# Queries, keys and values by 512 columns, one gate unit in each iteration of a recurrent mixer, and later sums of weights

## The chip, the cores and the metric

The kernel runs on one core of a Trainium2 chip. A core has five engines that work side by side: TensorE (PE) multiplies matrices, VectorE (DVE) and ScalarE (ACT) work elementwise, GpSimd (POOL) does some elementwise work and issues copies, SyncE (SP) issues most transfers. TensorE's weight loads (PEld) are recorded apart from its matmuls (PE). The metric is the device time of one execution in microseconds (us), lower is better.

## The reference, cut to what matters

One sequence of 1024 tokens of width 1024 goes through two layers in float32.

```python
def recurrent_mixer(hn, w_in, conv_w, conv_b, ..., w_out):
    z = hn @ w_in                                   # 1024 -> 2 * 1408
    gate, xr = jnp.split(z, 2, axis=-1)
    xr = causal_depthwise_conv(xr, conv_w, conv_b)
    y = rg_lru(xr, gate_a_w, ..., lam)              # 16 blocks of 88 channels
    return (y * jax.nn.gelu(gate)) @ w_out

def rg_lru(x, w_a, b_a, w_x, b_x, lam):
    r = jax.nn.sigmoid(einsum("bsnd,nde->bsne", xb, w_a) + b_a)
    i = jax.nn.sigmoid(einsum("bsnd,nde->bsne", xb, w_x) + b_x)
    a = jnp.exp((-LRU_C * r) * jax.nn.softplus(-lam))
    u = sqrt(-expm1(2 * log_a)) * (i * x)           # then h[t] = a[t] h[t-1] + u[t]

def shared_kv(h, c_act, ...):
    hn = modulate(rms_norm(h, kv_norm_g), shift, scale)
    k, v = jnp.split(hn @ kv_w, 2, axis=-1)         # 1024 -> 2 * 1024, k normalised per head

def chunk_attention(hn, w_q, ...):
    q = rms_norm((hn @ w_q).reshape(...), q_norm_g) # 1024 -> 1024
    ...                                             # 16 chunks of 64 against 9 chunks of keys
    return out @ w_o

def sqrelu_mlp(hn, w1, w2):
    return jnp.square(jax.nn.relu(hn @ w1)) @ w2    # 1024 -> 4096 -> 1024
```

Layer 0 is the recurrent mixer and an MLP; then keys and values are formed from the residual stream; layer 1 is attention and an MLP. Shifts, scales and gates of both layers ("modulation") come from a product of one vector with large weights (`ada_w`, `kv_ada_w`).

## The kernel before, in words

**Precision.** Every large product is three matmuls, recorded at lines L329 to L331 in `mm3`: high times high, high times low, low times high. Each float32 operand is split into a high half by a copy on ScalarE (L196 for weights and reloaded activations) and the rest by a subtraction on VectorE (L200).

**The stream of weights.** A class `Stream` (`ws`) keeps one list of items in the order in which they are wanted. Loads are issued on SyncE's queue in that order, into a ring of seven raw buffers of 128x1024 (`ws.ns`). Items for TensorE (`to="w"`) are split into tiles `wh` and `wl`; there are eight such tiles, so four items can be split at a time (`cap["w"] = 8`). `ws.next()` gives the next split item, `ws.done()` frees its tiles and lets the next be split. Items of kind "a" are reloaded activations whose halves are tiles of 128x512; `cap["a"]` bounds how many of these may be held. Items of kind "u" are the modulation weights: each 128x1024 tile is multiplied with the vector and summed by one VectorE instruction (L362); `some(n)` puts n of them into the list. Items of kind "p" form sums of four quarter weights for the MLP (L126), some on VectorE, some on GpSimd.

**Two ways of order.** Queries, keys and values, and attention, are ordered by an automatic scheduler from the program's order and its dependencies. The mixer and both MLPs are ordered by hand: `tick()` counts steps of TensorE (12 matmuls of 512 columns in the mixer), `at(d, f)` puts work d ticks later, and `ws.lag[kind]` is how many ticks after a load was issued its first use is put into the program.

**The mixer.** The width of 1408 is 11 tiles (`NT`) of 128 channels. `xr(t)` projects tile t of the recurrent half (two halves of 512 tokens, 8 k-steps, 3 matmuls each: 48 matmuls), then the convolution (L924), copies of channel blocks on GpSimd (L932), and splits on ScalarE (L938) and VectorE (L945) follow some ticks later. `gate(t)` projects tile t of the gate half, also 48 matmuls. `recur(_done(t))` does the blocks of 88 channels that end in tile t: block products (12 matmuls of 88x512 for each block), sigmoids (L971), tanh, roots and exponentials on ScalarE, and multiplies and the scan on VectorE (L976, L995 to L1002). The scanned block goes to a tile of 128 channels by a transfer, is multiplied with its gate (L1015, `gated`), stored to DRAM (`ygd`) and loaded back as a split item.

The main loop over t = 4 to 10 runs `xr(t)`, `recur(_done(t - 1))` and a gate unit, except at t = 8, where no gate unit runs; gate units 8 and 9 come at t = 9 and 10, gate unit 10 and the last blocks' `recur` after the loop. The splits of a tile come a tick later where `late` holds (tiles 3 to 9 except 8).

**Output projection.** For each j of 4 output pairs, `part_of` multiplies the weights `w_out(0, j)` with three gated tiles and `w_out(1, j)` with four, for two halves of tokens and two output tiles: four banks, 36 and then 48 matmuls. Then `chunk` adds the last four gated tiles for all outputs. `cap["a"]` is 14 from the last gate unit on.

**MLP.** The first product is 16 steps p of seven products of quarter matrices; partial results are added on VectorE (L1263) in the first and L1285 in the second product. At step (13, 0) `ws.lag["p"]` goes from 4 to 2 ticks.

**Queries, keys and values.** Tokens are stationary (128 tokens by 128 k) and weights stream by 256 columns. One item holds four k-steps of 256 columns; a group is 256 output columns, two items. A bank of 128x512 holds two token tiles of one group. For queries' first two groups the two first token halves run k by k in four banks while the normalisation of the rest (`head`, L556 to L585) goes on; all else runs bank by bank. `tokens_out` copies a bank in two pieces of 128x256 (L1392), and for queries and keys squares it (L1395) and reduces it per head (L1396). `kvmodulate` forms the keys' and values' operand from the residual stream in three parts between query groups.

Of the kernel before, what the change touches and what calls it, by code (L numbers as in the profile page):

```python
# [10 lines left out]
AF = mybir.ActivationFunctionType  # L11
ALU = mybir.AluOpType
# [4 lines left out]
KD = 8  # L17
W = 1408
NT = 11
# [284 lines left out]
def trunk(ctx: ExitStack, tc: tile.TileContext, I, out, dbg=None, stop=None):  # L304
# [107 lines left out]
    for t in range(4, NT):  # L412
        w_in(NT + t)
        some({8: 3, 9: 2, 10: 3}.get(t, 0))
        gate_item(_done(t - 1))
        if t != 8:
            w_in(t if t < 8 else t - 1)
    w_in(NT - 1)
    gate_item(_done(NT - 1))
# [89 lines left out]

    mlp_units(0)  # L510
    for g in range(4):
        for kk in range(2):
            ws.add(I["wq"][g * 2 + kk], 1024)
    for g in range(8):
        for kk in range(2):
            ws.add(I["wkv"][g * 2 + kk], 1024)
        some(4)
    some(99)
# [430 lines left out]
    def conved(t):  # L949

        conv(t)
        at(1, copies, t)
        late = 2 < t < NT - 1 and t != 8
        at(4 if late else 3, split_hi, t)
        at(5 if late else 4, split_lo, t)
# [112 lines left out]
    gate(3)  # L1068
    for t in range(4, NT):
        xr(t)  # L1070
        recur(_done(t - 1))
        if t != 8:
            gate(t if t < 8 else t - 1)
    ws.cap["a"] = 14
    gate(NT - 1)
    recur(_done(NT - 1))
    h = []
# [25 lines left out]
    for j in range(4):  # L1103
# [4 lines left out]
        for c, ys in enumerate((ygits[:3], ygits[3:7])):  # L1108
            for ps, (half, e) in zip(pss, chunks):
                part_of(ps, its[c], e, half, ys, c == 0, c == 1)  # L1110
                if c:
                    into_h(2 * j + e, half, ps)
                elif j == 0 and half == 0:
                    load_h(2)
                tick()
            at(1, ws.done, its[c])
    ws.live["a"] -= 14
    ws.cap["a"] = 8
# [45 lines left out]
    def mlp_body(l, h, nrm, nxt, last):  # L1164
# [88 lines left out]
        for p in range(2, 16):  # L1253
# [14 lines left out]
            def after(x, p=p, ca=ca, cb_=cb_):  # L1268
                ws.run()
                if x == 6:  # L1270
                    store(p, ca, cb_)
                if (p, x) == (13, 0):
                    ws.lag["p"] = 2
# [113 lines left out]

    def tokens_out(dst, sq, g, t2, ps):
        tt = slice(2 * t2, 2 * t2 + 2)
        for e in range(2):  # L1390
            d = dst[2 * g + e].rearrange("p (t c) -> p t c", t=8)[:, tt, :]
            A_.activation(out=d, in_=ps[:, :, e * 128 : (e + 1) * 128], func=AF.Copy)  # L1392
        if sq is not None:
            t = slot()
            A_.activation(out=t[:, :HALF], in_=ps.rearrange("p a b -> p (a b)"), func=AF.Square)  # L1395
            V.tensor_reduce(  # L1396
                out=ssq[:, sq, tt, 4 * g : 4 * g + 4],
                in_=t[:, :HALF].rearrange("p (t n d) -> p t n d", t=2, n=4),
                axis=AX, op=ALU.add)

    def token_mm(ps, N, its, t2, e, k, start, stop):
        q = slice((2 * t2 + e) * 128, (2 * t2 + e + 1) * 128)
        it = its[k // 4]
        c = slice((k % 4) * 256, (k % 4) * 256 + 256)
        mm3(ps[:, e, :], N.hh[k][:, q], N.hl[k][:, q], it["hi"][:, c], it["lo"][:, c], start, stop)

    def tokens(dst, N, sq, g, its, half):

        for t2 in range(2 * half, 2 * half + 2):
            ps = bank((128, 2, 256))  # L1410
            for e in range(2):
                for k in range(KD):
                    token_mm(ps, N, its, t2, e, k, k == 0, k == KD - 1)
            tokens_out(dst, sq, g, t2, ps)

    def tokens2(dst, N, sq, g):
        its = [ws.next() for _ in range(2)]
        for half in range(2):
            tokens(dst, N, sq, g, its, half)
        for it in its:  # L1420
            ws.done(it)

# [3 lines left out]

    its = [[ws.next() for _ in range(2)] for _ in range(2)]
    todo = [(g, t2, bank((128, 2, 256))) for g in range(2) for t2 in range(2)]
    for k in range(KD):
        for g, t2, ps in todo:  # L1430
            for e in range(2):
                token_mm(ps, n3, its[g], t2, e, k, k == 0 and e == 0, k == KD - 1 and e == 1)
        head(k, n3)
    for g, t2, ps in todo:
        tokens_out(qt, 0, g, t2, ps)
    for g in range(2):
        tokens(qt, n3, 0, g, its[g], 1)
        for it in its[g]:
            ws.done(it)
    kvmodulate((0, 1, 2))  # L1440
    tokens2(qt, n3, 0, 2)
    kvmodulate((3, 4, 5))
    tokens2(qt, n3, 0, 3)
    kvmodulate((6, 7))
    kt_ = [slot() for _ in range(8)]
    for g in range(4):
        tokens2(kt_, KV, 1, g)
    rqk = cp.tile([128, 2, 8, 16], F32, name="rqk")
# [23 lines left out]
    vt = [slot() for _ in range(8)]  # L1472
    for g in range(4):
        tokens2(vt, KV, None, g)
        if g < 2:
            head_norms(g, (qt, kt_)[g])
    dump("q", qt)
# [239 lines left out]
def layouts(inputs):  # L1717
# [61 lines left out]
    def grouped(w):  # L1779
        u = units(w, 4, 256)  # L1780
        n = u.shape[0] // 2
        return np.stack([u[:n], u[n:]], 1).reshape(2 * n, 128, 1024)

# [32 lines left out]
```

## Time and profile before

| | |
|---|---|
| median of 3 executions | 2364.78 us (2363.08 to 2367.6) |
| the profiled execution's own time | 2363.05 us |
| its span in the profile | 2361.2 us |
| mean granted TensorE clock | 0.991 |
| PE / PEld / DVE / ACT / POOL busy, of the span | 96 / 82 / 74 / 53 / 17% |
| mixer with its output projection | 0 to about 484 us |
| first MLP | to 1119.6 us |
| queries, keys, values | 1119.6 to 1399.6 us |
| attention and its output projection | to about 1730 us |
| second MLP | to the end |

A group in the profile reads: line, engine, operation, what is written from what is read, shape, count, then total busy time and the mean in ns of one, then the idle time of that engine just before such instructions and what ended it. In a timeline, each row has its start, its length and, in brackets, idle time before it with the instruction that ended the wait. A matmul's recorded length contains its way through the array; what counts for throughput is the distance between starts.

### The profile page before, as it was taken

To read this page: it belongs to the slowest core of one execution; us is meant where nothing else is said; L and a number is where in the kernel's file an instruction comes from. 1 tells how busy PE (TensorE), PEld (TensorE's weight loads), DVE (VectorE), ACT (ScalarE), POOL (GpSimd) and SP (SyncE) were. 2 spreads that over 40 slices of the span, in tenths; PEclk is the share of its full clock that TensorE was granted. 3 is DMA by queue.
4 is the path that set the end of the run, shared out by engine and by line. 5 is a ranking of instruction groups with operands and counts; after the bars stand their busy time and mean duration, and the time that the engine had idled before them with its cause. 6 is when DMAs were issued, how large, how long until landed. Compare 5 with 4: busy or idle time off the path is not lost.

```text
span 2361.2 us, 31725 instructions
## 1 busy us (share of the span) xinstructions
PE 2272.8 (96%) x11740; PEld 1929.1 (82%) x11740; DVE 1749.7 (74%) x2580; ACT 1240.2 (53%) x2051; POOL 399.2 (17%) x419
## 2 busy tenths in 40 slices
PE   3999999999999899999999999999999999999999
PEld 2878787878887678888999999998888888778887
DVE  8688889588777877777764739996386565877775
ACT  5587883375555633344433239996275555634332
POOL 0000100000000033331000148874000000033332
PEclk9999899999999999999999999999999999999999
DMA  8225349226676865545444100014114445865543
GB/s 314 72 83 155 116 158 340 99 85 231 245 257 225 306 224 155 159 159 185 124 134 143 55 12 11 10 53 143 67 54 160 162 170 172 288 237 160 153 150 130
DMA packets 141639, 363.46 MB, mean 154 GB/s; under 512 B 14924, under 2 KB 17100, under 8 KB 141484
## 3 DMA queue, kind: packets, MB, share of 16 engines
q1 hardware_dynamic: 113756, 278.45, 35.5%
q10 hardware_dynamic: 23824, 71.44, 8.1%
q0 software_dynamic: 3904, 11.54, 1.9%
q8 instruction: 92, 1.51, 0.3%
q14 instruction: 63, 0.52, 0.1%
HBM read 260.19 MB, written 89.65 MB: 148 GB/s over the span
## 4 chain that ended last, share of the span: by engine, by line
PE 63%; DVE 9%; DMA 8%; ACT 7%; issue 3%; POOL 1%; ACTq 0%; SPq 0%; DVEq 0%; POOLq 0%
PE b L329 20%; PE b L331 20%; PE b L330 20%; DMA hid<-s 2%; DMA ws<-in_w_dram 2%; DMA ws<-hid 2%; ACT s L1592 2%; PE b L1622 1%; DVE wl L200 1%; ACT s L334 1%; DVE s L200 1%; PE b L1641 1%; PE b L1642 1%; DMA s<-s 1%; DVE s L1181 1%
## 5 line engine op out<-in xcount | busy, mean ns | idle before, releaser
L329 PE MATMUL b<-s,wh 128*128 128x512 f32 (+1 forms) x2532 | 999.7, 395 | 36.7 <-DVE s L1285 12.5
L330 PE MATMUL b<-s,wh 128*128 128x512 f32 (+1 forms) x2532 | 994.4, 393 | 9.5 <-DVE s L817 5.3
L331 PE MATMUL b<-s,wl 128*128 128x512 f32 x2296 | 901.1, 392 | 2.9 <-DVE wl L200 2.9
L329 PEld LDWEIGHTS b<-s,wh 128*128 128x128 f32 (+1 forms) x2532 | 477.4, 189 | 153.2 <-DVE s L1263 11.5
L330 PEld LDWEIGHTS b<-s,wh 128*128 128x128 f32 (+1 forms) x2532 | 477.8, 189 | 115.6 <-DVE s L817 6.3
L196 ACT ACTIVATE wh<-ws 128x1024 fp32r<-128x1024 f32 (+3 forms) x302 | 290.7, 972 | 474.7 <-POOL ws L126 266.7
L331 PEld LDWEIGHTS b<-s,wl 128*128 128x128 f32 x2296 | 432.8, 189 | 98.0 <-DVE wl L200 4.6
L200 DVE TENSOR_TENSOR wl<-ws,wh 128x1024 fp32r<-128x1024 f32 (+1 forms) x249 | 303.0, 1220 | 136.4 <-ACT wh L196 134.0
L200 DVE TENSOR_TENSOR s<-ws,s 128x512 fp32r<-128x512 f32 x284 | 226.1, 812 | 8.1 <-ACT s L196 8.1
L1285 DVE SCALAR_TENSOR_TENSOR s<-b,mod,s 128x512 f32<-128x512 f32 x221 | 164.5, 745 | 77.5 <-PE b L331 77.2
L126 POOL TENSOR_TENSOR ws<-ws 128x512 f32<-128x512 f32 x21 | 27.1, 1291 | 1138.8 <-DMA s<-hsp 456.0
L329 PE MATMUL b<-wh,s 128*128 128x256 f32 x768 | 216.4, 284 | 0.0
L330 PE MATMUL b<-wl,s 128*128 128x256 f32 x768 | 215.9, 283 | 0.0
L331 PE MATMUL b<-wh,s 128*128 128x256 f32 x768 | 214.9, 283 | 0.4 <-DVE s L585 0.4
L196 ACT ACTIVATE s<-ws 128x512 fp32r<-128x512 f32 x284 | 164.2, 618 | 58.3 <-DMA ws<-hid 27.0
L329 PEld LDWEIGHTS b<-wh,s 128*128 128x128 f32 x768 | 147.1, 192 | 0.3 <-issue 0.2
L330 PEld LDWEIGHTS b<-wl,s 128*128 128x128 f32 x768 | 147.1, 192 | 0.3 <-issue 0.2
L331 PEld LDWEIGHTS b<-wh,s 128*128 128x128 f32 x768 | 146.3, 192 | 0.7 <-DVE s L585 0.7
L362 DVE CUSTOM_DVE_ANT_0 ws<-ws,cb,vec 128x1024 f32<-128x1024 f32 x59 | 75.1, 1280 | 70.3 <-DMA ws<-in_ada_dram 67.4
L1263 DVE TENSOR_TENSOR s<-s,b 128x512 f32<-128x512 f32 x84 | 57.2, 682 | 73.6 <-PE b L331 61.6
L1392 ACT ACTIVATE s<-b 128x256 f32<-128x256 f32 x96 | 31.6, 384 | 123.2 <-PE b L331 112.9
L1261 ACT ACTIVATE s<-b 128x512 f32<-128x512 f32 x84 | 50.0, 595 | 87.2 <-PE b L331 86.1
(165 smaller groups left out, 3064.4 us busy)
## 6 DMA issues: line engine op xcount, KB each, us to landing
hid<-s ACTq DMA_DIRECT2D x128, 512.0 KB, 4.9
ws<-hid SPq DMA_DIRECT2D x118, 512.0 KB, 4.6
ws<-in_w_dram SPq DMA_DIRECT2D x220, 256.0 KB, 3.6
ws<-in_ada_dram SPq DMA_DIRECT2D x56, 512.0 KB, 4.3
s<-in_ada_dram SPq DMA_DIRECT2D x40, 512.0 KB, 8.2
ws<-in_w_in_dram SPq DMA_DIRECT2D x22, 512.0 KB, 7.3
hsp<-s SPq DMA_DIRECT2D x32, 256.0 KB, 2.0
s<-hsp SPq DMA_DIRECT2D x16, 512.0 KB, 7.9
```

The costliest lines, as they stand in the source:

```text
L126: eng.tensor_tensor(out=out, in0=in0, in1=in1, op=op)
L196: self.nc.scalar.activation(out=hi[:rows, :n], in_=src, func=AF.Copy)
L200: self.nc.vector.tensor_tensor(out=lo[:rows, :n], in0=src, in1=hi[:rows, :n].bitcast(F32), op=ALU.subtract)
L329: PE.matmul(ps, ah, bh, start=start, stop=False, skip_group_check=more)
L330: PE.matmul(ps, ah, bl, start=False, stop=False, skip_group_check=more)
L331: return PE.matmul(ps, al, bh, start=False, stop=stop, skip_group_check=more).ins
L362: V.tensor_tensor_reduce(out=t, in0=t, in1=cb, op0=ALU.mult, op1=ALU.add, scale=1.0, scalar=bias, accum_out=dst)
L1261: A_.activation(out=t, in_=ps, func=AF.Copy)
L1263: V.tensor_tensor(out=t, in0=t, in1=ps, op=ALU.add)
L1285: V.scalar_tensor_tensor(out=t, in0=ps, scalar=g2[:, m : m + 1], in1=t, op0=ALU.mult, op1=ALU.add)
L1392: A_.activation(out=d, in_=ps[:, :, e * 128 : (e + 1) * 128], func=AF.Copy)
L1592: A_.activation(out=p[:, lo:640], in_=p[:, lo:640], func=AF.Exp, scale=-1.0, bias=m, accum_out=s1)
```

## The change: what it does

1. **Queries, keys and values.** Weights are stored so that an item holds two k-steps of 512 columns. A group is 512 output columns, four items, and runs in two halves of four token tiles; each half fills four banks k by k, with 512-wide matmuls. There are 1152 of them in place of 2304 with 256 columns. An item is freed after an odd k of the second half. A bank is copied in four pieces of 128x128. `kvmodulate` runs in two parts. In the list of items eight modulation items follow each group of four, where four followed two; the head norms of queries and keys follow the first and the second value group.
2. **Mixer.** `gate(t)` runs in every iteration from 4 to 10. `cap["a"]` goes to 6 before `xr(10)` and to 14 before `gate(10)`. `late` holds for all tiles from 3 on. The last blocks' `recur` runs after the output projection's first pair (j = 0). The list of items follows the new order.
3. **Sums of weights.** `ws.lag["p"]` goes to 2 at step (15, 0) in both MLPs.

```diff
         gate_item(_done(t - 1))
-        if t != 8:
-            w_in(t if t < 8 else t - 1)
-    w_in(NT - 1)
+        w_in(t)
     gate_item(_done(NT - 1))
...
+    for g in range(2):
+        for i in range(4):
+            ws.add(I["wq"][g * 4 + i], 1024)
     for g in range(4):
-        for kk in range(2):
-            ws.add(I["wq"][g * 2 + kk], 1024)
-    for g in range(8):
-        for kk in range(2):
-            ws.add(I["wkv"][g * 2 + kk], 1024)
-        some(4)
+        for i in range(4):
+            ws.add(I["wkv"][g * 4 + i], 1024)
+        some(8)
...
-        late = 2 < t < NT - 1 and t != 8
+        late = t > 2
...
     for t in range(4, NT):
+        if t == NT - 1:
+            ws.cap["a"] = 6
         xr(t)
         recur(_done(t - 1))
-        if t != 8:
-            gate(t if t < 8 else t - 1)
-    ws.cap["a"] = 14
-    gate(NT - 1)
-    recur(_done(NT - 1))
+        if t == NT - 1:
+            ws.cap["a"] = 14
+        gate(t)
...
             at(1, ws.done, its[c])
+        if j == 0:
+            recur(_done(NT - 1))
...
-                if (p, x) == (13, 0):
+                if (p, x) == (15, 0):
                     ws.lag["p"] = 2
...
+    def tokens_out(dst, sq, g, t, ps):
+        for p in range(4):
+            A_.activation(out=dst[4 * g + p][:, t * 128 : (t + 1) * 128],
+                          in_=ps[:, p * 128 : (p + 1) * 128], func=AF.Copy)
+        if sq is not None:
+            x = slot()
+            A_.activation(out=x[:, :HALF], in_=ps, func=AF.Square)
+            V.tensor_reduce(out=ssq[:, sq, t, 8 * g : 8 * g + 8],
+                            in_=x[:, :HALF].rearrange("p (n d) -> p n d", n=8), axis=AX, op=ALU.add)
+
+    def tokens(dst, N, sq, g, more=None):
+
+        its = [ws.next() for _ in range(4)]
+        for half in range(2):
+            pss = [bank() for _ in range(4)]
+            for k in range(KD):
+                it, c = its[k // 2], slice((k % 2) * HALF, (k % 2) * HALF + HALF)
+                for t, ps in enumerate(pss):
+                    q = slice((4 * half + t) * 128, (4 * half + t + 1) * 128)
+                    mm3(ps, N.hh[k][:, q], N.hl[k][:, q], it["hi"][:, c], it["lo"][:, c], k == 0,
+                        k == KD - 1)
+                if half == 0 and more:
+                    more(k)
+                if half and k % 2:
+                    ws.done(it)
+            for t, ps in enumerate(pss):
+                tokens_out(dst, sq, g, 4 * half + t, ps)
...
+    tokens(qt, n3, 0, 0, lambda k: head(k, n3))
+    kvmodulate((0, 1, 2, 3))
+    tokens(qt, n3, 0, 1)
+    kvmodulate((4, 5, 6, 7))
+    kt_ = [slot() for _ in range(8)]
     for g in range(2):
-        tokens(qt, n3, 0, g, its[g], 1)
...
+        tokens(kt_, KV, 1, g)
...
+    for g in range(2):
+        tokens(vt, KV, None, g)
+        head_norms(g, (qt, kt_)[g])
...
     def grouped(w):
-        u = units(w, 4, 256)
-        n = u.shape[0] // 2
-        return np.stack([u[:n], u[n:]], 1).reshape(2 * n, 128, 1024)
+
+        u = units(w, 2, 512)
+        return u.reshape(4, -1, 128, 1024).transpose(1, 0, 2, 3).reshape(-1, 128, 1024)
```

More of the change, by code (lines that the diff above doesn't have):

```diff
@@ L1386, in trunk @@
     ssq = cp.tile([128, 2, 8, 16], F32, name="ssq")
[L1388 to L1392, printed above, removed]
-        if sq is not None:
[L1394 to L1414, printed above, removed]
@@ L1416, in tokens2 @@
-    def tokens2(dst, N, sq, g):
-        its = [ws.next() for _ in range(2)]
-        for half in range(2):
-            tokens(dst, N, sq, g, its, half)
-        for it in its:
-            ws.done(it)
+    def tokens_out(dst, sq, g, t, ps):
+        for p in range(4):
+            A_.activation(out=dst[4 * g + p][:, t * 128 : (t + 1) * 128],
+                          in_=ps[:, p * 128 : (p + 1) * 128], func=AF.Copy)
+        if sq is not None:
+            x = slot()
+            A_.activation(out=x[:, :HALF], in_=ps, func=AF.Square)
+            V.tensor_reduce(out=ssq[:, sq, t, 8 * g : 8 * g + 8],
+                            in_=x[:, :HALF].rearrange("p (n d) -> p n d", n=8), axis=AX, op=ALU.add)
@@ L1425, in kvmodulate @@
             modulate(KV, ks, half, h, n3.r, aa[:, 32:40], kvmod[:, 0:8])
[L1427 to L1435, printed above, removed]
-    for g in range(2):
-        tokens(qt, n3, 0, g, its[g], 1)
[L1438 to L1447, printed above, removed]
+    tokens(qt, n3, 0, 0, lambda k: head(k, n3))
[3 more added lines that the diff above has]
+    kt_ = [slot() for _ in range(8)]
+    for g in range(2):
+        tokens(kt_, KV, 1, g)
     rqk = cp.tile([128, 2, 8, 16], F32, name="rqk")
@@ L1472, in trunk @@
     vt = [slot() for _ in range(8)]
[L1473 to L1476, printed above, removed]
+    for g in range(2):
+        tokens(vt, KV, None, g)
+        head_norms(g, (qt, kt_)[g])
     dump("q", qt)
```

## The prediction

> **What bounds the kernel now.** I read the page's busy row first, then the groups of instructions for queries, keys and values, then the timeline and windows around each place that the change touches.
>
> ```profile
> PE 2272.8 (96%) x11740; PEld 1929.1 (82%) x11740; DVE 1749.7 (74%) x2580; ACT 1240.2 (53%) x2051; POOL 399.2 (17%) x419
> ...
> L329 PE MATMUL b<-wh,s 128*128 128x256 f32 x768 | 216.4, 284 | 0.0
> L330 PE MATMUL b<-wl,s 128*128 128x256 f32 x768 | 215.9, 283 | 0.0
> L331 PE MATMUL b<-wh,s 128*128 128x256 f32 x768 | 214.9, 283 | 0.4 <-DVE s L585 0.4
> ```
>
> TensorE is busy for 96% of the span, so matmul time and the few pauses between matmuls set the time. The 768 × 3 = 2304 matmuls of 256 columns are the whole of queries, keys and values; almost no idle time stands before them. So that stage is worth its number of matmuls times their spacing, which the timeline shows where the widths meet:
>
> ```profile
> 1118.00 0.39 PE L331 MATMUL b<-s,wl 128*128 128x512 f32 x1
> ...
> 1119.36 0.39 PE L331 MATMUL b<-s,wl 128*128 128x512 f32 x1
> 1119.59 0.28 PE L329 MATMUL b<-wh,s 128*128 128x256 f32 x1
> ...
> 1122.46 0.28 PE L330 MATMUL b<-wl,s 128*128 128x256 f32 x1
> 1122.58 0.28 PE L331 MATMUL b<-wh,s 128*128 128x256 f32 x1
> 1122.70 0.28 PE L329 MATMUL b<-wh,s 128*128 128x256 f32 x1
> ```
>
> From 1118.00 to 1119.59 seven 512-wide matmuls start: 1.59 / 7 = 0.227 us each. The 256-wide ones start 0.120 us apart. Twice 0.120 is 0.013 more than 0.227: half the width does not take half the time.
>
> In the mixer the bound changes for a moment. These are TensorE's timeline at two pauses, then windows (length, then busy us and count of PE, PEld, DVE, ACT, POOL, then granted clock):
>
> ```profile
> 282.29 0.62 PE L329 MATMUL b<-s,wh 88*88 88x512 f32 x1 [2.53 <-ACT s L938]
> 283.55 0.73 PE L330 MATMUL b<-s,wh 88*88 88x512 f32 x1 [0.64 <-DVE s L945]
> ...
> 296.02 0.44 PE L329 MATMUL b<-s,wh 128*128 128x512 f32 x1
> ...
> 366.45 0.50 PE L329 MATMUL b<-s,wh 128*128 128x512 f32 x1 [0.60 <-ACT wh L196]
> ...
> 368.39 0.50 PE L331 MATMUL b<-s,wl 128*128 128x512 f32 x1 [1.21 <-DVE wl L200]
> ```
>
> ```profile
> 282.30:296.00 13.70, 13.06 (x30) 8.32 (x31) 11.26 (x10) 10.87 (x15) 0.54 (x1) 0.51 0.13 34
> 265.90:354.80 88.90, 85.73 (x349) 66.32 (x348) 77.03 (x72) 73.41 (x93) 9.41 (x18) 0.92 0.45 141
> 387.00:406.00 19.00, 19.00 (x86) 15.73 (x85) 18.86 (x31) 5.38 (x8) 0.00 (x0) 1.00 1.01 389
> 406.00:425.00 19.00, 19.00 (x86) 15.73 (x85) 10.09 (x14) 4.11 (x5) 0.00 (x0) 1.00 0.52 188
> ```
>
> At 282 the gates' block products wait for the splits of convolved tile 8, and after these pauses TensorE runs at a granted clock of 0.51: 30 matmuls in 13.70 us where 30 × 0.227 = 6.8 would do. The loss is 2.5 + 6.9 = 9.4 us. At 366 the output projection waits for its weights' halves, 0.60 and 1.21 idle; with what each first matmul takes longer that is about 2.1 us.
>
> **The change, part by part.**
>
> *Queries, keys, values.* Matmuls of 256 columns go (2304 × 0.120 = 276.5 us), half as many of 512 columns come. The trace shows 512-wide ones only with weights stationary; here the tokens are. Both widths have the same 128x128 load in front. Bounds: 1152 × 0.227 = 261.5 (like the 512-wide rows) and 276.5 (no gain). I take 261.5, the row of the same width: −15.0.
>
> Evacuation: 192 copies of 128x128 replace 96 of 128x256, the squares and reductions stay.
>
> ```profile
> L1392 ACT ACTIVATE s<-b 128x256 f32<-128x256 f32 x96 | 31.6, 384 | 123.2 <-PE b L331 112.9 <-issue 9.5 <-DVE s L585 0.6
> L1395 ACT ACTIVATE s<-b 128x512 f32<-128x512 f32 x32 | 19.3, 614 | 0.0
> ...
> L196 ACT ACTIVATE wh<-ws 128x1024 fp32r<-128x1024 f32 x20 | 21.2, 1062 | 25.6 <-PE b L330 25.6
> ...
> L200 DVE TENSOR_TENSOR wl<-ws,wh 128x1024 fp32r<-128x1024 f32 x22 | 27.4, 1268 | 1.5 <-ACT wh L196 1.5
> ```
>
> ```profile
> 1398.50 0.28 PE L331 MATMUL b<-wh,s 128*128 128x256 f32 x1
> 1399.58 1.06 PE L1538 MATMUL b<-ident,dk 128*128 128x128 f32 x8 [0.80 <-ACT s L1392]
> ...
> 1398.82 0.66 ACT L1392 ACTIVATE s<-b 128x256 f32<-128x256 f32 x2 [5.10 <-PE b L331]
> 1265.52 1.46 SPq L159 DMA_DIRECT2D ws<-in_wkv_dram  x2
> 1269.18 15.98 SPq L159 DMA_DIRECT2D ws<-in_ada_dram  x4
> ```
>
> Two 128x256 copies in a row take 0.66, so 0.28 from start to start; a 128x128 one lies between 0.14 and 0.28. Four banks end together now: 16 copies and 4 squares, at most 16 × 0.28 + 4 × 0.61 = 6.9 us, under the next half's 96 × 0.227 = 21.8 us of matmuls in the other four banks. ScalarE waited 112.9 us for TensorE here, so they cost nothing there. Only the last half of the values has no cover: attention's first transpose waits 0.80 us now for two copies; the four banks finish 3 × 0.227 = 0.68 apart, so 16 copies of 0.14 to 0.28 (2.2 to 4.5) overhang by 0.4 to 2.5. I take +1.0 more than now (0 to +1.9).
>
> Weights: a group now holds all eight tiles of split weights, so the next group's cannot be split ahead of it. Each item is freed at an odd k of the second half; the next group needs the same item 16.4 us later (72 × 0.227). The split is 1.06 + 1.27 = 2.3, with the evacuation ahead of it 9.2 us: hidden; without the cover up to 9.2 per group. On SP's queue eight modulation units stand between groups instead of twice four. Their loads are issued (15.98 − 0.33) / 3 = 5.2 us apart where one buffer rotates. I cost this at nothing: the seven buffers let a group's loads go ahead of its splits. The price if not is a rival below. The first group's second half needs its normalised tokens k by k (2.7 us each) where one token tile formerly needed all eight k within 24 matmuls; its one wait, 0.4, does not grow. Sum for the stage: −15.0 + 1.0 = **−14.0** (−15.0 to −13.1, 0 at worst spacing).
>
> *Mixer.* Gate unit 8 now runs between recurrent unit 8 and recurrent unit 9, where before nothing stood: 48 more matmuls, 10.9 us, ahead of the block products that waited until 282.3. They would have run at 279.4 and were late by about 4 us with both halves. The splits of tiles 8 and 10 also come one tick later, twelve matmuls or 2.7 us (tile 10's products move behind other work): 6.7 of 10.9. So the 9.4 go. Total matmuls are the same.
>
> But the last blocks' products, 24 matmuls, move from ahead of the output projection's start into its first quarter. In the row 265.90:354.80 TensorE reaches the second part of the first quarter (its weights' low half ended at 354.7). Without the 9.4 loss and without 24 × 0.227 = 5.4 it is there at 354.8 − 14.8 = 340.0. VectorE did 77.0 us of work in that row; of it only two multiplies of the last blocks (1.2 each) are not needed there, 74.6 are. Started at 265.9 and never idle, it has the halves at 340.5. It idled 88.9 − 77.0 = 11.9, of which 2.4 in the 282.30 window and about 2 just ahead are the stall itself; 7.5 lie outside. So the pause is between 0.5 (idle used up) and 8.0 (all kept); I take the middle, 4.3, since three early splits are allowed two units sooner. The 2.1 at 366 go with it, as that pause came from the same backlog. Pauses of this size have a second price. At 282, 2.53 and 0.64 brought 6.3 of slow clock on top of the idle; this is how a longer one in the MLP stands:
>
> ```profile
> 799.54 0.80 PE L329 MATMUL b<-s,wh 128*128 128x512 f32 x1 [4.42 <-DVE s L1263]
> 800.14 0.63 PE L330 MATMUL b<-s,wh 128*128 128x512 f32 x1
> 800.56 0.63 PE L331 MATMUL b<-s,wh 128*128 128x512 f32 x1
> ...
> 804.40 0.53 PE L331 MATMUL b<-s,wh 128*128 128x512 f32 x1
> ```
>
> Eleven matmuls in 4.86 us, 2.4 lost. Between 2.4 and 6.3 I take 4.3 (0 to 6.3). Late next are the last blocks' gated tiles for the final third of the projection: they start about 13 us later, on a VectorE that is full until 406 (18.86 of 19.0) and has 8.9 us free before 425, when they are needed; 0 to +4, I take 0. Sum: −9.4 − 2.1 + 4.3 + 4.3 = **−2.9** (−11.0 to +6.8).
>
> *Sums of weights.* During hidden steps 13 and 14 of each MLP the shorter lag made VectorE wait for a load in front of the sums, and TensorE wait behind it in the first MLP:
>
> ```profile
> 749.79 0.69 DVE L126 TENSOR_TENSOR ws<-ws 128x512 f32<-128x512 f32 x1 [4.13 <-DMA ws<-in_w_dram]
> ...
> 756.72 0.50 PE L329 MATMUL b<-s,wh 128*128 128x512 f32 x1 [1.78 <-DVE s L1263]
> ...
> 1987.76 0.69 DVE L126 TENSOR_TENSOR ws<-ws 128x512 f32<-128x512 f32 x1 [1.95 <-DMA ws<-in_w_dram]
> ```
>
> ```profile
> 1980.00:2000.00 20.00, 20.00 (x90) 16.57 (x89) 13.03 (x19) 10.75 (x17) 0.00 (x0) 1.00 0.49 170
> ```
>
> Two ticks later the load has landed: −1.9 with the slower first matmul. Behind the sums on VectorE's queue stand the operands L1263 and the splits; put off, they may crowd the 4.42 at 799.54, so +4 to −4. In the second MLP VectorE's wait of 1.95 delayed no matmul (TensorE is busy for all of the 20.00 us around it): 0. Sum **−1.9**.
>
> Profiled execution before: 2363.05, span 2361.2. 2363.05 − 14.0 − 2.9 − 1.9 = 2344.3. The median shown, 2364.78, is 1.7 above the profiled one; I add it: **2346**.
>
> A rule of the Trainium skill speaks against the first part: "TensorE: Matmul & The Clock Gate", section "Wait — 56ns, not 53.3ns?", has warm matmuls start N / 2.4 + 2.5 ns apart, 109 for 256 columns and 216 for 512. By it the stage would gain only 2304 × 0.109 − 1152 × 0.216, about 3 us, and the whole come to about 2358. The rows' 120 and 227 ns do not agree with it; the rows decide.
>
> **Rivals.** For the last of them, the modulation units' group and the loads of the weights between 1200 and 1300:
>
> ```profile
> L362 DVE CUSTOM_DVE_ANT_0 ws<-ws,cb,vec 128x1024 f32<-128x1024 f32 x17 | 21.8, 1283 | 46.1 <-DMA ws<-in_ada_dram 46.1
> ```
>
> ```profile
> ws<-in_wkv_dram SPq DMA_DIRECT2D x8, 512.0 KB, 3.7
> ```
>
> 1. *VectorE closes up* at the opening of the output projection: the pause is 0.5, no slow clock, −11.0 in the mixer: 2363.05 − 14.0 − 11.0 − 1.9 + 1.7 = 2338. For it: 11.9 us of idle VectorE. Against: it needs nearly all of them. 22%.
> 2. *The stall moves whole*: 8.0 + 6.3 + 4 − 11.5 = +6.8, and the sums bring nothing: 2363.05 − 14.0 + 6.8 + 1.7 = 2358. For it: VectorE full through 387 to 406. Against: the pause only follows from gaps that need not recur. 13%.
> 3. *The change does not do what it says*: 512-wide matmuls with stationary tokens keep 0.240, as both halves wait on the same weight-load path (PEld 82%). Gain 0 + 1.0: 2363.05 + 1.0 − 2.9 − 1.9 + 1.7 = 2361. Against: PEld's loads are halved too. 4%. The page's rule above, 2358, shares this chance.
> 4. *Slower: the weights of a group come late*. Place: starts of the second key group and both value groups. Eight modulation loads at 5.2 are 41.6, four weight loads of 1.46 − 0.33 = 1.1 each 4.5, the last one's landing 3.7 and its split 2.3: 52.1 against 192 × 0.227 = 43.6 of a group's matmuls, so 8.5 late three times, each with 6.3 of slow clock: 3 × 14.8 = 44: 2346 + 44 = 2390. It decides from (18.8 + 4.7) / 3 = 7.8 us per group. For it: VectorE waited 46.1 us for the modulation loads. Against: no matmul waited for weights there, and the buffers load ahead. 5%.
>
> **How the numbers follow.** The forecast has 56%; its own range, with the mixer from −7 to +1, is 2342 to 2350. Rival 1 takes the range down to 2336 and rival 2 up to 2358; outside are rivals 3 and 4 and the tails of 1 and 2, about 2 in 10. What can be told from no change is 0.2%, 4.7 us: under 2360 is faster. Forecast, rival 1 and most of 2: 0.88; the rest of 2 and rival 3: 0.07; rival 4: 0.05.
>
> **What would show it.** The stage: 1152 matmuls 128x512 from tokens, 0.227 apart, and attention's first transpose some 264 us after the stage's start. The mixer: the granted clock whole at 282, a pause before the output projection's second weights released by VectorE's split, and the length of the slow clock after it. The sums: no wait for a load in front of L126 at step 13, and 1.8 less idle there. The forecast falls if the 512-wide spacing exceeds 0.235, if TensorE waits for splits at group starts, or if the opening costs under 2 or over 12 us.

## The result, and the profile after

The changed kernel takes 2350.4 us in the median of 5 executions (2346.2 to 2353.2), the kernel before 2364.3 (2360.9 to 2367.6). The ratio is 0.9941 with an interval of 0.9925 to 0.9957, so 13.9 us less (10.2 to 17.7). 2346 with a range of 2336 to 2358 was predicted: the direction and the range hold, the gain is 5 us smaller than the 18.8 forecast. Two more comparisons of the same kernel, in the experiments, gave 16.5 and 10.3 us less.

The page of the changed kernel's profile: its span and busy row, and from the groups of its stage for queries, keys and values (columns as before: busy time, mean ns of one, idle before and its releaser) TensorE's matmuls, VectorE's modulation units and ScalarE's copies:

```profile
span 2350.0 us, 29512 instructions
...
PE 2258.7 (96%) x10588; PEld 1871.9 (80%) x10588; DVE 1751.7 (75%) x2580; ACT 1246.2 (53%) x2148; POOL 397.1 (17%) x419
```

```profile
L330 PE MATMUL b<-wl,s 128*128 128x512 f32 x384 | 149.9, 390 | 0.0
L329 PE MATMUL b<-wh,s 128*128 128x512 f32 x384 | 148.9, 389 | 0.0
L331 PE MATMUL b<-wh,s 128*128 128x512 f32 x384 | 146.4, 389 | 1.1 <-DVE s L584 1.1
...
L362 DVE CUSTOM_DVE_ANT_0 ws<-ws,cb,vec 128x1024 f32<-128x1024 f32 x35 | 44.8, 1283 | 32.8 <-DMA ws<-in_ada_dram 26.1 <-DMA ws<-in_kvada_dram 6.2
...
L1391 ACT ACTIVATE s<-b 128x128 f32<-128x128 f32 x192 | 39.0, 346 | 84.5 <-PE b L331 82.4 <-PE b L330 2.0
```

TensorE has 1152 matmuls fewer and is as full as it was. To see where the 11.2 us between the two spans went, I take four places that both traces have: the first 512-wide matmul of the normalisation after the mixer (the one that spreads its factors over the partitions), the first of queries, keys and values, attention's first transpose, and its last product with the values. Two of the four were shown for the kernel before (1119.59 and 1399.58); its other two, and then all four of the changed kernel, from the timelines of TensorE:

```profile
458.79 1.02 PE L567 MATMUL b<-s,ones 128*128 128x512 f32 x2
...
1631.64 0.28 PE L1642 MATMUL b<-s,v 128*128 128x256 f32 x1
```

```profile
459.48 1.02 PE L566 MATMUL b<-s,ones 128*128 128x512 f32 x2
...
1118.00 0.39 PE L329 MATMUL b<-wh,s 128*128 128x512 f32 x1
...
1383.43 1.06 PE L1517 MATMUL b<-ident,dk 128*128 128x128 f32 x8 [0.92 <-ACT s L1391]
1385.13 1.09 PE L1517 MATMUL b<-ident,dq 128*128 128x128 f32 x8 [0.63 <-POOL dq L1507]
...
1620.70 0.28 PE L1621 MATMUL b<-s,v 128*128 128x256 f32 x1
```

| stage | before | changed | difference | predicted |
|---|---|---|---|---|
| mixer, to the normalisation | 458.8 | 459.5 | +0.7 | −2.9 |
| rest of the mixer's layer, first MLP | 660.8 | 658.5 | −2.3 | −1.9 |
| queries, keys, values | 280.0 | 265.4 | −14.6 | −14.0 |
| attention | 232.1 | 237.3 | +5.2 | 0 |
| the rest, to the span's end | 729.6 | 729.3 | −0.3 | 0 |

So two of the three parts came in as sized. Of the difference to the forecast, 3.6 us are the mixer, and 5.2 are a stage in which I had expected nothing; the other three stages together took 1.3 less than forecast. (These two executions lie 11.2 apart, the medians 13.9.)

**The mixer.** Windows of the changed kernel (length; busy time and count of PE, PEld, DVE, ACT and POOL; granted clock; the last two are DMA share and GB/s) and TensorE's pauses at the opening of the output projection:

```profile
265.90:340.60 74.70, 74.70 (x329) 59.81 (x327) 64.62 (x60) 61.70 (x78) 8.13 (x16) 1.00 0.48 148
338.00:360.00 22.00, 13.48 (x44) 9.74 (x43) 19.81 (x25) 8.32 (x11) 1.04 (x2) 0.69 1.00 365
```

```profile
342.56 0.50 PE L330 MATMUL b<-s,wh 128*128 128x512 f32 x1 [1.81 <-DVE s L200]
349.47 0.79 PE L330 MATMUL b<-s,wh 128*128 128x512 f32 x1 [5.95 <-DVE s L200]
351.88 0.80 PE L330 MATMUL b<-s,wh 128*128 128x512 f32 x1 [0.76 <-DVE s L200]
```

From 265.9 to 340.6 TensorE is busy throughout at full clock: the pause at 282 and its slow clock are gone. But then it waits 1.81 + 5.95 + 0.76 = 8.5 us for VectorE's lower halves of gated tiles, and the clock falls after it: 44 matmuls in 22.00 us, where 44 × 0.227 = 10.0 would do, 12.0 lost. 11.5 had been taken away.

**Attention.** Its first 25 us in the kernel before and in the changed one:

```profile
1399.60:1424.60 25.00, 21.69 (x163) 19.77 (x164) 19.68 (x55) 22.41 (x54) 21.36 (x28) 1.00 0.04 11
```

```profile
1383.40:1408.40 25.00, 19.23 (x129) 16.93 (x129) 17.12 (x45) 18.58 (x44) 23.40 (x34) 0.93 0.04 11
```

163 matmuls have become 129, and GpSimd is the fuller engine (23.40 of 25). The reason stands ahead of attention, on VectorE and GpSimd. First the kernel before:

```profile
1349.48 13.65 DVE L1466 TENSOR_TENSOR s<-s,rqk 128x1024 f32<-128x1024 f32 x8
...
1350.87 1.88 POOL L1523 TENSOR_SCALAR dk<-s 128x1024 f32<-128x1024 f32 x1 [279.65 <-DVE s L1466]
...
1396.27 0.42 POOL L1492 MEMSET s<- 128x384 f32 x1 [24.07 <-PE b L331]
```

Then the changed one:

```profile
1369.93 12.97 DVE L1446 TENSOR_TENSOR s<-s,rqk 128x1024 f32<-128x1024 f32 x8
...
1371.33 1.88 POOL L1502 TENSOR_SCALAR dk<-s 128x1024 f32<-128x1024 f32 x1 [0.77 <-DVE s L1446]
...
1381.80 2.01 POOL L1502 TENSOR_SCALAR dk<-s 128x1024 f32<-128x1024 f32 x1
1383.78 1.30 POOL L1507 TENSOR_TENSOR dq<-s,dq 128x512 fp32r<-128x512 f32 x1
```

The keys' eight multiplies of the head norms start 50 us ahead of attention before, and 13.5 us ahead of it in the changed kernel, because they follow "the second value group", which was the middle and is now the end. GpSimd's copies of keys and queries for attention's first heads hang on them. Before, GpSimd had finished them and idled 24 us; now it is at work on them when attention starts, and TensorE's second transpose already waits for it (`POOL dq`, 0.63 above).

### The profile page after: what moved, and what is told of

Its sections match the earlier page's. It is cut to its first block, busy times and chain, and to the rows that moved or that the text cites. A ratio compares the mean times of both kernels' runs of the same rounds, so it can differ in the third digit from the quotient of the medians.

```text
span 2350.0 us, 29512 instructions
## 1 busy us (share of the span) xinstructions
PE 2258.7 (96%) x10588; PEld 1871.9 (80%) x10588; DVE 1751.7 (75%) x2580; ACT 1246.2 (53%) x2148; POOL 397.1 (17%) x419
## 4 chain that ended last, share of the span: by engine, by line
PE 68%; DVE 10%; DMA 10%; ACT 6%; issue 3%; POOL 2%; ACTq 0%; SPq 0%; POOLq 0%; DVEq 0%
PE b L329 21%; PE b L330 21%; PE b L331 21%; DMA hid<-s 4%; DMA ws<-in_w_dram 3%; DMA ws<-hid 2%; DVE wl L200 2%; PE b L1601 1%; ACT s L1571 1%; DVE s L200 1%; DVE s L1182 1%; ACT s L334 1%; POOL ws L126 1%; PE b L1620 1%; PE b L1621 1%
## 5 line engine op out<-in xcount | busy, mean ns | idle before, releaser
L330 PEld LDWEIGHTS b<-s,wh 128*128 128x128 f32 (+1 forms) x2532 | 478.0, 189 | 124.3 <-DVE s L200 10.1
L330 PE MATMUL b<-wl,s 128*128 128x512 f32 x384 | 149.9, 390 | 0.0
L329 PE MATMUL b<-wh,s 128*128 128x512 f32 x384 | 148.9, 389 | 0.0
L331 PE MATMUL b<-wh,s 128*128 128x512 f32 x384 | 146.4, 389 | 1.1 <-DVE s L584 1.1
L331 PE MATMUL b<-s,wh 128*128 128x512 f32 x236 | 92.5, 392 | 0.0
L335 DVE TENSOR_TENSOR s<-b,s 128x384 fp32r<-128x384 f32 x144 | 82.7, 593 | 12.1 <-ACT s L334 11.6
L1576 POOL TENSOR_SCALAR s<-s,sm 128x640 f32<-128x640 f32 (+4 forms) x128 | 86.1, 685 | 22.3 <-DVE sm L1574 22.3
L1571 ACT ACTIVATE s<-s,sm 128x640 f32<-128x640 f32 (+4 forms) x128 | 88.3, 696 | 1.6 <-DVE sm L1569 1.6
```

Of the source, the lines that this page charges most:

```text
L329: PE.matmul(ps, ah, bh, start=start, stop=False, skip_group_check=more)
L330: PE.matmul(ps, ah, bl, start=False, stop=False, skip_group_check=more)
L331: return PE.matmul(ps, al, bh, start=False, stop=stop, skip_group_check=more).ins
L335: V.tensor_tensor(out=lo, in0=src, in1=hi.bitcast(F32), op=ALU.subtract)
L1571: A_.activation(out=p[:, lo:640], in_=p[:, lo:640], func=AF.Exp, scale=-1.0, bias=m, accum_out=s1)
L1576: G.tensor_scalar(out=p[:, lo:640], in0=p[:, lo:640], scalar1=sm[:, 4 + e : 5 + e], scalar2=1.0, op0=ALU.mult, op1=ALU.mult)
```

## The experiments

Every ratio below is to the kernel before, run beside it on the same chip. Differences in us are those of the medians, except in the first table, where they go with the ratios.

**The three parts alone.** The edits are the three parts of the diff shown above, each applied alone to the kernel before.

> The kernel before with only the part for queries, keys and values. The changed kernel's trace has this stage 14.6 us shorter and attention 5.2 us longer, so my theory (the stage gives the gain and attention's start gives part back) expects 9 to 10 us less than before, about 2355 where before is 2364, with attention from its first transpose to its last product again near 237 us where before has 232. The rival, that attention's extra time comes from something else in that run, expects about 14.6 less, 2349 to 2350.

> The kernel before with only the mixer's part. Theory (the stall only moves: 9.4 and 2.1 us go, 9.2 of idle and about 4.4 of slow clock come at the opening of the output projection): within 2 us of before, with TensorE waiting for VectorE's splits for 7 to 10 us between 335 and 355 us. My prediction's value would be 2.9 less; the rival that VectorE closes up would be 11 less.

> The kernel before with only the later sums of weights. Theory: 2 to 2.5 us less, and the pause of TensorE at 756.7 gone. The rival (sums put off crowd what follows) expects no gain: the pause at 799.5 longer by as much.

| part alone | ratio | interval | us |
|---|---|---|---|
| queries, keys, values | 0.9965 | 0.9952 to 0.9977 | −8.3 (−11.3 to −5.4) |
| mixer | 1.0005 | 0.9997 to 1.0014 | +1.2 (−0.7 to +3.3) |
| later sums | 0.9997 | 0.9988 to 1.0006 | −0.7 (−2.8 to +1.4) |

The first part shows the changed kernel's picture: its stage is 14.5 us shorter than before, attention 5.2 longer, and attention's first 25 us are the same row almost digit for digit:

```profile
1385.70:1410.70 25.00, 19.24 (x128) 16.91 (x129) 17.04 (x45) 18.55 (x44) 23.31 (x34) 0.93 0.04 11
```

So attention's loss belongs to this part and is no accident of one run. The mixer alone brings nothing, and its trace has the moved pause with neither of the other parts present:

```profile
344.04 0.50 PE L330 MATMUL b<-s,wh 128*128 128x512 f32 x1 [2.26 <-DVE s L200]
350.96 0.80 PE L330 MATMUL b<-s,wh 128*128 128x512 f32 x1 [5.95 <-DVE s L200]
353.36 0.79 PE L330 MATMUL b<-s,wh 128*128 128x512 f32 x1 [0.76 <-DVE s L200]
```

For the sums the time alone does not tell: the interval holds both my 2 to 2.5 and nothing. The trace does show the mechanism. VectorE's wait of 4.13 in front of the sums has become 0.19, and TensorE has no pause at that place:

```profile
747.23 0.69 DVE L126 TENSOR_TENSOR ws<-ws 128x512 f32<-128x512 f32 x1 [0.19 <-DMA ws<-in_w_dram]
```

Over all the traces of this study the stretch from the normalisation to queries, keys and values takes 660.8, 660.1 and 658.9 us in the three with the early switch of the lag, and 653.8 to 660.9, in the mean of eleven 657.0, in those with the late one. That is 3.0 less, with a scatter as large. The rival, that the 4.42 us at 799.5 grows by as much, is not what the traces show: 2.9 there in this run, with a second pause of 2.8 behind it where before had 0.48, so 0.8 more in all.

The three add up to 8 us less, and the whole gave 10 to 17. The intervals of the parts, 2 to 3 us wide on each side, leave room for most of that; whether the parts help each other is open.

**The keys' norms.**

```diff
-        head_norms(g, (qt, kt_)[g])
+        if g == 0:
+            head_norms(0, qt)
+            head_norms(1, kt_)
```

> The changed kernel, with the head norms of the keys ahead of the second value group in place of behind it. Theory: attention starts 4 us late in the changed kernel because the keys' eight multiplies on VectorE now run up to 1382.8, so that GpSimd's copies for the first heads are late and share its port; with the norms earlier this goes, 4 us less than the changed kernel, about 14 + 4 = 18 less than before. The rival (the sixteen copies of the last banks, or the slow clock by itself, make the start late) expects the same time as the changed kernel.

The ratio was 0.9940 (0.9926 to 0.9954), 15.3 less than before: not the 18 that I had expected, and hardly more than the 13.9 of the changed kernel in its own comparison. So the two were run again side by side on one chip.

> The changed kernel a third time, so that the next two stand beside it on one chip: 13 to 17 us less than before.

> The changed kernel with the keys' norms ahead of the second value group, as before it, now beside the changed kernel on one chip. By the traces attention is 4.4 us shorter, so 3 to 5 us less than the changed kernel; the rival (the gain is given back in what follows) expects the same time.

There the changed kernel has 0.9955 (0.9939 to 0.9971), 2352.6 us, and the one with earlier norms 0.9929 (0.9916 to 0.9942), 2346.1 us: 6.5 us less, where 3 to 5 were expected; the changed kernel itself was only 10.3 less than before, under the 13 to 17 expected. The intervals overlap slightly, so the time alone would leave some doubt; the trace does not. Attention's first 25 us with earlier norms:

```profile
1378.40:1403.40 25.00, 21.67 (x163) 19.75 (x164) 19.67 (x55) 22.38 (x53) 21.34 (x28) 1.00 0.03 7
```

163 matmuls at full clock again, as in the kernel before, and attention takes 232.8 us. The wait for ScalarE's copies of the last banks, 0.92 us, is still there in that trace, so the sixteen copies are not what made attention late. Nor is the slow clock the first cause: over all fourteen traces attention takes 232.1 to 234.8 us in the ten whose keys' norms come early, and 237.3, 237.3, 237.3 and 240.1 in the four with the late ones. But it has a share. The 234.8 is the run with only the later sums, where 3.4 us of half clock, so 1.7 lost, came behind attention's first waits without any late norms.

In the run beside it the changed kernel's attention took 240 us, with one wait of 3.91 us for VectorE where the first trace had 1.15. Of the four traces with late norms it is the only one so long, so part of the 6.5 us may be this run's own.

> The changed kernel itself once more, on the same chip as the next three: 13 to 15 us less than before, attention again some 237 us.

This earlier repeat of the changed kernel, on another chip, gave 0.9933 (0.9921 to 0.9945), 16.5 less: a little more than expected, with attention at 237.3. The changed kernel's three comparisons thus gave 13.9, 16.5 and 10.3 less than before, those with earlier norms 15.3 and 16.7: what the norms are worth is read more safely from attention's 4.4 to 4.5 us in the traces than from the times.

**What sets the pause at the output projection.** Three kernels, all with the earlier norms, so that they stand against the 15.3 and 16.7 us less than before of the norms alone. The first puts the last blocks back ahead of the output projection:

```diff
-        late = t > 2
+        late = 2 < t < NT - 1
...
         gate(t)
+    recur(_done(NT - 1))
...
-        if j == 0:
-            recur(_done(NT - 1))
```

> The changed kernel with the keys' norms earlier, and the last blocks' recurrence put back ahead of the output projection (its splits a tick earlier, as before). Theory (VectorE's backlog of about 9 us stands at the opening; 24 matmuls ahead of it cover 5.4 of this, for 2.4 more of VectorE's work): the pause before the second weights falls from 9.3 to 4 to 7 us, and 2 to 5 us less than the changed kernel with earlier norms, at least 4 less than the changed kernel alone. The rival (moving the last blocks made no pause, the gate unit order did) expects the pause unchanged.

0.9942 (0.9931 to 0.9954), 14.1 less: nothing gained. The pause did not shrink, it moved to the last blocks' products:

```profile
340.07 0.73 PE L329 MATMUL b<-s,wh 88*88 88x512 f32 x1 [8.40 <-ACT s L937]
341.33 0.73 PE L330 MATMUL b<-s,wh 88*88 88x512 f32 x1 [0.53 <-DVE s L944]
```

My theory's number falls: the 24 matmuls do not cover anything, since they wait for the same backlog (the splits of tile 10). The stated rival fits the size, but its wording, that the gate units' order made the pause, is only half of it, as the next two show. The second allows all fourteen split halves one unit earlier:

```diff
         if t == NT - 1:
-            ws.cap["a"] = 6
+            ws.cap["a"] = 14
         xr(t)
         recur(_done(t - 1))
-        if t == NT - 1:
-            ws.cap["a"] = 14
```

> The changed kernel with the keys' norms earlier, and all fourteen split halves allowed from the last recurrent unit on in place of six. Theory: VectorE idles 6.5 us at 304 to 310 and the lower halves of tiles 3 to 6 come 20 us later; allowed earlier, they use such gaps and the pause of 9.3 falls by 3 to 6 us. The rival (VectorE is simply full from 310 on, and ScalarE's splits wait on its own queue) expects the pause to stay within 1.5 us.

0.9937 (0.9922 to 0.9951), 15.3 less. The pause at the opening fell from 8.5 to 5.2 us, by 3.3 where the theory gave 3 to 6 (what the expectations call 9.3 is 8.0 to 9.0 in the traces of this mixer), but now for the weights' upper half on ScalarE, and a new one came 70 us later:

```profile
344.74 0.79 PE L329 MATMUL b<-s,wh 128*128 128x512 f32 x1 [5.16 <-ACT wh L196]
...
414.01 0.50 PE L331 MATMUL b<-s,wl 128*128 128x512 f32 x1 [2.77 <-DVE wl L200]
```

The third gives TensorE 36 more matmuls that need only tiles already split, by running the first parts of two output pairs ahead of the second part of the first:

```diff
-    for j in range(4):
...
-        for c, ys in enumerate((ygits[:3], ygits[3:7])):
+    for j, c in ((0, 0), (1, 0), (0, 1), (1, 1), (2, 0), (2, 1), (3, 0), (3, 1)):
...
+        if (j, c) == (0, 1):
+            recur(_done(NT - 1))
```

(the list of items follows this order).

> The changed kernel with the earlier norms, and in the output projection the first parts of two output pairs ahead of the second part of the first: 36 more matmuls, 8.2 us, that need only the first three gated tiles. Theory (the pause at the opening is elementwise work that is about 9 us behind; the cover decides, not the order of the gate units): the pause of 9.3 us falls to 1 to 3 and the slow clock of 4 us behind it goes, 6 to 11 us less than with the norms alone, and near 2336 to 2340. The rival (the backlog moves on to the next place where split weights or tiles are wanted) expects a gain under 3 us with new pauses between 350 and 425 us.

0.9952 (0.9938 to 0.9966), 11.3 less: 5 us worse than with the norms alone. At the opening the expected happened, 1.02 and 1.80 us of pause and no slow clock (granted 1.00 from 340 to 361). But then:

```profile
363.23 0.46 PE L329 MATMUL b<-s,wh 88*88 88x512 f32 x1 [0.84 <-DVE s L1101]
365.10 0.47 PE L329 MATMUL b<-s,wh 88*88 88x512 f32 x1 [0.94 <-DVE s L1101]
367.99 0.73 PE L329 MATMUL b<-s,wh 88*88 88x512 f32 x1 [1.96 <-ACT s L974]
```

```profile
427.75 0.50 PE L329 MATMUL b<-s,wh 128*128 128x512 f32 x1 [1.81 <-ACT wh L196]
429.00 0.74 PE L331 MATMUL b<-s,wl 128*128 128x512 f32 x1 [0.53 <-DVE wl L200]
```

The four banks of the second pair stay taken, so the last blocks' products wait for banks to be emptied, and the last third's weights come late. Behind these pauses the clock is halved, for 10.2 us from 367.7 and 3.4 from 429.1. The rival, that the backlog moves on, was right; it had not expected a loss.

**The mixer as before, and a gap one iteration later.** Both with the earlier norms, the later sums and the wide matmuls. The second leaves out the gate unit at t = 9 in place of t = 8:

```diff
-        if t != 8:
-            gate(t if t < 8 else t - 1)
+        if t != 9:
+            gate(t if t < 9 else t - 1)
```

(the list of items and `late` follow).

> The changed kernel with the keys' norms earlier and the mixer as before. Theory (the mixer's part brought nothing: a stall of 9.4 and one of 2.1 went, 13 to 14 came): the same time as the changed kernel with earlier norms within 2 us, some 18 less than before; the pauses at 282 and 366 are back. My prediction's mixer term expects it 2.9 slower than with the new mixer.

> The queries', keys' and values' part, the later sums and the earlier norms, with the mixer as before except that the iteration without a gate unit is t = 9 in place of t = 8. Recurrent unit 9 finishes one block, unit 8 two, so the splits that the block products wait for are one copy (1.06 us) and one subtraction (1.22) shorter. Theory (the total of elementwise work between 266 and 355 us sets the opening; the gap in the gate units only chooses where TensorE waits): the pause and slow clock at 282 shrink from 9.4 to 2 or less at about 293 to 310, and 2 to 7 us of new pause stand before the output projection's second weights; net 1 to 5 us less than with the old mixer, near 2341 to 2345 where before is 2364. The rival (the backlog takes all of it) expects the same as with the old mixer.

The old mixer has 0.9925 (0.9914 to 0.9937), 2345.1 us, 18.8 less than before; the gap at t = 9 has 0.9922 (0.9908 to 0.9936), 2344.9 us, 18.4 less. In the old mixer's trace the pauses are back, 2.56 and 0.62 us at 283 and 0.57 and 1.25 at 368. The changed kernel beside it (2347.4) differs in the norms too, so it does not tell the mixers apart; the two kernels beside it that have the same norms and a new mixer, those with the last blocks ahead and with the early splits, took 2349.8 and 2348.6, so 4.7 and 3.5 more. The new mixer as it is in the changed kernel, with earlier norms, was 15.3 and 16.7 less than before, with intervals that overlap the old mixer's. And over the traces the stretch to the normalisation takes 459.3 us in the mean of four with the old mixer and 459.9 in six with the changed kernel's. The prediction's mixer term, 2.9 in favour of the new mixer, has no support; the mixer alone, between 0.7 less and 3.3 more, excludes it. The gap at t = 9 did not shrink the pause, it carried it along, and the rival, the same time as with the old mixer, was right:

```profile
312.54 0.73 PE L329 MATMUL b<-s,wh 88*88 88x512 f32 x1 [3.83 <-ACT s L939]
313.79 0.73 PE L330 MATMUL b<-s,wh 88*88 88x512 f32 x1 [0.53 <-DVE s L946]
```

Six arrangements of the same mixer, six places of the pause (282; 312; 340; 342 to 352; 344 and 414; spread from 345 to 429), and none gains more than the runs can tell. The best times found, wide matmuls with the norms ahead of the second value group and the old mixer with its gap at t = 8 or at t = 9, are faster than the kernel before by 18 to 19 us.

## Why the prediction was right or wrong

**The wide matmuls: right.** From 1118.00 the 512-wide matmuls start 0.23 us apart, and a window in the middle of the stage has 443 of them in 100 us (0.226):

```profile
1200.00:1300.00 100.00, 100.00 (x443) 82.81 (x442) 57.51 (x85) 39.60 (x118) 0.00 (x0) 1.00 0.47 148
```

The row of the same width was the right one to take, stationary tokens or not. By the rule of the Trainium skill ("TensorE: Matmul & The Clock Gate", section "Wait — 56ns, not 53.3ns?") the gain would have been about 3 us (2.3 with the prediction's rounded figures); it was 14.6, and the rows before had already shown that two 256-wide matmuls take 13 ns more than one of 512. The copies at the end cost less than the 1.0 taken: 0.92 of wait where 0.80 stood, inside the bounds; the 0.63 behind it is GpSimd's. Splits never held up a group. The normalisation's wait in the first group grew from 0.4 to 1.1, where I had said that it would not. Rivals 3 and 4 did not come.

**Attention: missed.** The step that failed is the list of what moves in the first part. I costed the copies, the weights and the modulation units, and put the head norms at nothing without a word: the description of the change says that they follow the first and the second value group, and with groups twice as large the second group's end is the stage's end. The work is the same; its cover, half of the values' matmuls, went, and behind it stand GpSimd's copies for attention. The rows that would have told it were in the trace before: VectorE's eight multiplies at 1349.48 and GpSimd's idle 24 us. 5.2 us between the two traces, of which the earlier norms give back 4.4 to 4.5.

**The mixer: the mechanism right, the pause twice its size.** I had the pause between 0.5 and 8.0 with 4.3 taken, and slow clock up to 6.3 with 4.3 taken. 8.5 us of pause came, above the upper bound, and 3.5 of slow clock, 12.0 in all, on the very edge of what I had named as the sign that the forecast falls (over 12): rival 2's pause, with about half of its slow clock and without its further 4 in the last third. The wrong step was to take the middle, 4.3, for the pause, on the ground that VectorE's idle time can be used up. The trace after shows what its idle time is made of. VectorE did 64.62 us of work from 265.9 to 340.6 and idled 10.1, more than the 7.5 that I let it keep at most. The largest piece:

```profile
302.61 1.21 DVE L975 TENSOR_TENSOR s<-s,s 88x1024 f32<-88x1024 f32 x1
310.34 1.22 DVE L944 TENSOR_TENSOR s<-s,s 88x1024 fp32r<-88x1024 f32 x1 [6.52 <-ACT s L937]
```

It waits for a split on ScalarE. VectorE does nothing else meanwhile, and ScalarE is at work on what stands ahead of the split in its own order, the block functions and two loads of their tables:

```profile
302.56 1.28 ACT L987 ACT_TABLE_LOAD   x1
303.86 2.01 ACT L987 ACTIVATE s<-s 88x1024 f32<-88x1024 f32 x2
305.87 1.28 ACT L990 ACT_TABLE_LOAD   x1
307.17 2.19 ACT L990 ACTIVATE s<-s,sp 88x1024 f32<-88x1024 f32 x2
309.26 1.05 ACT L937 ACTIVATE s<-s 88x1024 fp32r<-88x1024 f32 x1
```

Such idle time belongs to a chain that alternates between two engines, each with its work in a fixed order; it is no reserve. The table loads alone are 2.56 of the 6.52 us. Leaving out a wait of TensorE does not shorten that chain, and the wait came back wherever TensorE next asked for its results; that the chain's length sets the pause is argued from the six arrangements, and no kernel with a shorter chain (fewer table loads, or the split ahead of the block functions) was run. The part of the sentence on early splits did come true when they were allowed earlier still (5.2 in place of 8.5), and brought no time.

**The later sums: right in the trace, not told by the time.** The wait for the load and the pause at 756.7 are gone; −2.3 in the changed kernel against −1.9; alone it measured −0.7 with an interval of 2 on each side.

**The sum.** −14.6, +0.7, −2.3 against −14.0, −2.9, −1.9, and +5.2 that was not in the sum. That 2350.4 still lies in the range is partly luck: the width was given for the mixer (−11.0 to +6.8), and it took in an error in attention that nothing in the prediction allowed for. The forecast's own range, 2342 to 2350, was just missed, on rival 2's side.

## What to carry to other kernels

When a loop's groups become larger, look up everything that is placed "after group n": it moves with the group, and its cover goes; in this case 4 to 5 us of attention went that way and came back with a change of three lines. Idle time of an engine that works in order counts as reserve only if its next instruction is ready; look at what ended it before you let it fill up. And a pause that several engines' backlog makes was not removed here by giving TensorE other work first: six orders of this mixer only chose the place. Making the backlog itself shorter is what remains to be tried.

## What the runs showed of the hardware

The length of the slow clock does not follow from the length of the pause. In the kernel before, 2.53 and 0.64 us of idle were followed by 30 slow matmuls and 4.42 by eleven; with the gap at t = 9, 3.83 and 0.53 by some nine us at a reduced clock (the first window below), and in the run with only the later sums 2.88 us at 794.6 (the second row) by none: the next matmuls start at their usual distance until the next pause, and the granted clock is 1.00 from 790 to 800:

```profile
309.00:323.00 14.00, 9.93 (x25) 6.81 (x26) 10.31 (x9) 12.10 (x16) 1.06 (x2) 0.63 0.05 10
```

```profile
794.57 0.50 PE L329 MATMUL b<-s,wh 128*128 128x512 f32 x1 [2.88 <-DVE s L1263]
```

In the clock records of all these traces the half clock lasts 3.4 us or a multiple of it: 3.4 from 800.3 in the run with the later sums, 6.8 from 797.9 in the kernel before, 10.2 from 311.6 with the gap at t = 9, 13.7 from 282.5 in the kernel before. The Trainium skill ("TensorE: Matmul & The Clock Gate", section "What's actually happening") has the gate watch a free-running window of about 3.4 us, which would make pauses of 2.5 to 4 us a matter of where they fall; the different outcomes here fit that. It has the full clock come back after at least one busy window; the 13.7 us at 282 are four. For a sum this means that a pause near 3 us can cost anything from nothing to some 7 us beside its own length.

VectorE's multiplies with the norms and GpSimd's copies of keys take longer where they run together: in the changed kernel 12.97 us for eight (1.62 each) and 1.7 to 2.0 for a copy, where with earlier norms the multiplies have a length of 1.22 each and the copies that come after them take 1.05 to 1.09. With earlier norms one copy of GpSimd, started while VectorE was in a row of such multiplies, is shown with a length of 22 us:

```profile
1325.09 22.32 POOL L1504 TENSOR_SCALAR dk<-s 128x1024 f32<-128x1024 f32 x1 [260.96 <-DVE s L1446]
1347.39 0.64 POOL L1507 TENSOR_SCALAR dq<-s 128x512 fp32r<-128x512 f32 x1
```

So there VectorE kept its pace and GpSimd stood; in the changed kernel both were slower. What decides between the two was not tested.
